# A chunk's second sums are cast behind the copy of its first product group, a half-down's last weights behind its two copies

## Chip, core and metric

One core of a Trainium2 chip runs the whole program. The metric is device microseconds (us) of one execution; the median of three runs of the kernel before is 1778.77 us (1778.58 to 1780.93).

## What is computed

A decoder trunk of two layers on 512 tokens of width 1024, in float32. Each layer has a half-step SwiGLU FFN, a mixer (gated linear attention in the first layer, stick-breaking attention in the second) and another half-step FFN; a final norm ends it. So there are four FFNs, and the change is in them alone:

```
def swiglu(h, w_gate, w_up, w_down):
    return (jax.nn.silu(h @ w_gate) * (h @ w_up)) @ w_down
...
    x = x + 0.5 * swiglu(rmsnorm(x, ffn1_norm[i]), ffn1_w_gate[i], ffn1_w_up[i], ffn1_w_down[i])
```

The inner width is 2816.

## The kernel before

**Splitting.** A float32 product is made of three passes: each operand is split into a high part (a cast to fp32r, on ScalarE, ACT) and a low part (operand minus high part, on VectorE, DVE), and TensorE (PE) multiplies high by high, low by high, high by low. For weights the cast is line 138 and writes `wh`, the subtraction is line 139 and writes `wl`. Both have four buffers of 128x1024 each, taken in turn; a piece of 128x512 has buffers of its own.

**Chunks of seven products.** For most of the inner width a chunk of 256 weight columns is multiplied with Strassen's scheme in seven products instead of eight (`seven`, lines 708 to 820). A product is 12 matmuls with 256 moving columns. A chunk needs two kinds of sums of its weights, both made on DVE: the first sums `s12` (lines 718 and 719) and the second sums `s34` (lines 724 and 725). It is two entries of a work list, the *feed*. The first entry, `body_1`, has units a11 (128x512), s12 and a2 (128x1024 each) and four products: 1 with a11 into the PSUM tile `ps_w`; ACT copies that to `ps_z` (line 761, the **z copy**); 2 with s12 into `ps_q`; 3 with s12, added onto `ps_w`, so it may not begin before the z copy has read `ps_w`; 4 with a2, added onto `ps_z`. The second entry, `body_2`, has the unit s34 and three products: 5 with s34 onto `ps_w`, 6 with s34 onto `ps_q`, 7 with a2 onto `ps_w`. Products 5, 6 and 7 each wait until ACT has copied the earlier content out (lines 769 for 5, 765 for 6, 783 for 7). DVE or ACT then gate the result (lines 743 and 746), and it is split (lines 838 and 839).

**Downs and half-downs.** The product with `w_down` is cut into *downs* (`down`, one unit of 128x1024, 24 matmuls with 512 columns) or, for groups 1 and 3 of an FFN, into two *half-downs* each (`seven_down`, lines 358 to 454), which are seven products of two parts m=0 and m=1 with six matmuls each, 12 together. Their `body_1` has units a11 (128x512), s12 and a2 (128x1024, cast as two pieces of 128x512, `wh<-rawd`), and runs: w (a11 into `ps_w` of both m, each followed by a copy to `ps_z`, line 412: the **two copies**), q (s12), t2 (s12 onto `ps_w`, behind the copies; line 400 then adds it to x on DVE), z (first piece of a2 onto `ps_z`). `body_2` (s34): t3 onto `ps_w`, behind the addition of line 400 that reads it, then a copy of each m (line 439, `u3`); b22 onto `ps_q`; t4 (second piece of a2) onto `ps_w`, where m=0 waits for the first of those copies and m=1 for the second.

**Order of the feed in one FFN.** Call the chunks 1 to 18 and the half-downs A to D. The matmuls of an FFN run so, the first entries and the last downs left out: chunks 1, 2, 3, a down, 4, a down, 5, 6, half-down **A**, 7, 8, 9, half-down **B**, a down, 10, a down, 11, a down, 12, a down, 13, 14, half-down **C**, 15, 16, half-down **D**, a down, 17, 18, downs. In the first FFN chunk 2 begins at 73.44 us, chunk 6 at 122.66, A at 132.46, B at 170.7, C at 248.25, chunk 16 at 267.0, D at 277.1 and the down behind it at 286.6.

**Who decides the order.** The code asks for splits ahead of use: when an entry starts, `Feed.start` splits the units of that entry and of the next two, as long as they have at most four units of 128x1024 together, views the next four and issues loads for the next six. A scheduler then puts each engine's instructions into one order at build time, by priority; instructions made under `ahead()` get a higher one. Each engine takes its list in that order and waits at an instruction whose inputs are not there. Weights are loaded by SyncE (SP): `raw` (1 MB, two buffers) for chunks, `rawd` (512 KB, two buffers) for downs and half-downs. A half-down takes both `rawd` buffers, and the load of the next down's weights is issued when DVE has read the last piece of a2 from one of them (line 139).

Of the kernel before, what the change touches and what calls it, by code (L numbers as in the profile page):

```python
# [46 lines left out]
def decoder(ctx: ExitStack, tc: tile.TileContext, a: dict, out: bass.AP):  # L47
# [60 lines left out]
    class Entry:  # L108
# [12 lines left out]

        def split(self):
            if self.W is None:
                self.W = []
                for r, (_, _, n, m) in zip(self.view(), self.units):
                    few = n * m < 1024
                    if few:

                        h, l = (
                            st["few"].tile([P, n * m], F32R, tag="v" + t, bufs=1, name="w" + t) for t in "hl"  # L130
                        )
                    else:
                        h, l = (wp.tile([P, n * m], F32R, tag="w" + t, bufs=4, name="w" + t) for t in "hl")
                    h, l = (t.rearrange("p (n m) -> p n m", m=m) for t in (h, l))
                    pieces = r if isinstance(r, tuple) else (r,)
                    for i, part in enumerate(pieces):
                        k = slice(i * n // len(pieces), (i + 1) * n // len(pieces))
                        st["cut"] = nc.scalar.copy(h[:, k], part).ins  # L138
                        nc.vector.tensor_tensor(out=l[:, k], in0=part, in1=h[:, k].bitcast(F32), op=ALU.subtract)  # L139
                    self.W.append((h, l))  # L140

    class Feed:
# [49 lines left out]
    def ahead():  # L192

        return tc.high_priority(4000)
# [163 lines left out]
    def seven_down(pool, w, r0, hs, part):  # L358
# [43 lines left out]
        def body_1(W):  # L402
            a11, s, v["a2"] = W
            ws, zs, qs = [], [], []
# [3 lines left out]
            for m in range(2):  # L408


                zs.append(psum("ps_z")[:, 0:H])
                nc.scalar.copy(zs[m], ws[m])
            yield
# [37 lines left out]

        units = [(lower, lambda t: halves()[0], 2, 256), (lower, sums_12, 4, 256), (lower, lambda t: halves()[1::2], 4, 256)]
        feed.q.append(Entry(units, body_1))
        feed.q.append(Entry([(lower, sums_34, 4, 256)], body_2))

    def back_tok(w, r0, nf, hs, done):
# [160 lines left out]
    class FFN:  # L617
# [90 lines left out]
        def seven(self, ch, group=None):  # L708
# [41 lines left out]
            def body_1(W):  # L750
# [9 lines left out]
                with ahead():  # L760
                    nc.scalar.copy(z, w)  # L761
                yield
# [57 lines left out]
            feed.q.append(Entry(units, body_1))  # L820
            feed.q.append(Entry([(ch, sums_34, KD, P)], body_2))

        def t_half(self, i, j):
# [58 lines left out]
        def evac_u(self, ps, group):  # L882
            t = self.tp.tile([P, T], F32, tag="t", name="t")
            if not self.normed:
                nc.vector.tensor_tensor(out=pair(t), in0=flat(ps), in1=pair(st["R"]), op=ALU.mult)
            nc.vector.tensor_tensor(
                out=pair(t), in0=flat(ps) if self.normed else pair(t), in1=pair(self.gates.pop(0)), op=ALU.mult
            )
            self.close(t, group)

# [1045 lines left out]
```

## Time and profile before

| | |
|---|---|
| median of three runs | 1778.77 us |
| the profiled execution's own time | 1778.36 us |
| span of its instructions | 1776.4 us, 31377 instructions |
| PE busy | 1755.4 us, 99% |
| DVE busy | 1509.6 us, 85% |
| ACT busy | 1079.6 us, 61% |
| granted TensorE clock | 0.999 of full |

The execution's time is 1.94 us longer than its span. Busy means that at least one instruction is in flight; matmuls overlap, so PE counts as busy through most short delays, and delays are better seen in the rows of waits and in the length of a product. PEld is the loading of PE's weights, which runs beside the matmuls and waits for the same things.

### The profile page before, as it was taken

The page shows a single profiled execution, that of the slowest core. Times are in us where ns is not written, and L with a number is a line of the kernel's source. Part 1 is how long each engine was busy: PE and PEld are TensorE (multiplying, and loading weights), DVE is VectorE, ACT ScalarE, POOL GpSimd, SP SyncE. Part 2 cuts the span into 40 slices and gives each one's busy share as a digit, 9 for nine tenths or more (in the row PEclk, how much of TensorE's full clock was granted, in tenths as well). Part 3 has the DMA queues.
Part 4 walks back from the last instruction along what each step waited for, and adds up shares of the span by engine and source line. Part 5 has one row for each costly group of instructions (what it writes and reads, how often), then busy time and mean ns, then how long its engine had stood idle before and what let it go on. Part 6 is the DMA issues. An engine that isn't in the chain of part 4 may idle for free.

```text
span 1776.4 us, 31377 instructions
## 1 busy us (share of the span) xinstructions
PE 1755.4 (99%) x12714; PEld 1630.6 (92%) x12714; DVE 1509.6 (85%) x2474; ACT 1079.6 (61%) x1883; POOL 55.6 (3%) x77
## 2 busy tenths in 40 slices
PE   9999999999999999999999999999999999999998
PEld 8999999889888899999889999999888888999997
DVE  8999797786888989888798988967898679997986
ACT  7556556554655566555655555655888755565564
POOL 0000000200000000000000000010000000000000
PEclk9999999999999999999999999999999999999999
DMA  5543435422123433444434344342212234434441
GB/s 167 154 120 119 125 102 148 113 66 73 54 90 100 121 117 120 119 120 125 129 95 133 102 125 126 118 120 83 84 48 72 72 95 131 126 104 123 120 138 52
DMA packets 186388, 193.14 MB, mean 109 GB/s; under 512 B 4930, under 2 KB 171124, under 8 KB 186244
## 3 DMA queue, kind: packets, MB, share of 16 engines
q1 hardware_dynamic: 177760, 175.91, 31.7%
q0 software_dynamic: 8240, 14.95, 4.6%
q8 instruction: 99, 1.62, 0.4%
q14 instruction: 45, 0.37, 0.1%
q10 hardware_dynamic: 244, 0.29, 0.0%
HBM read 175.17 MB, written 2.10 MB: 100 GB/s over the span
## 4 chain that ended last, share of the span: by engine, by line
PE 60%; DVE 30%; ACT 5%; issue 3%; DMA 2%; SPq 0%; DVEq 0%; ACTq 0%
PE ps_w L733 13%; PE ps_d L80 12%; DVE wl L139 9%; PE ps_f L80 7%; PE ps_q L733 6%; PE ps_t L80 4%; PE ps_z L733 3%; PE ps_b L80 3%; PE ps_w L394 3%; ACT wh L138 2%; DVE x L400 2%; DVE hl L839 1%; PE ps_q L394 1%; DVE ts L848 1%; PE ps_z L1424 1%
## 5 line engine op out<-in xcount | busy, mean ns | idle before, releaser
L139 DVE TENSOR_TENSOR wl<-raw,wh 128x1024 fp32r<-128x1024 f32 x241 | 255.5, 1061 | 59.4 <-ACT wh L138 58.8
L138 ACT CAST wh<-raw 128x1024 fp32r<-128x1024 f32 x241 | 221.6, 920 | 77.8 <-PE ps_f L80 22.6
L139 DVE TENSOR_TENSOR wl<-s,wh 128x1024 fp32r<-128x1024 f32 x176 | 214.6, 1219 | 50.7 <-ACT wh L138 50.7
L733 PE MATMUL ps_w<-th,wh 128*128 128x256 f32 x864 | 239.4, 277 | 6.3 <-ACT ps_z L761 6.3
L733 PE MATMUL ps_w<-th,wl 128*128 128x256 f32 x864 | 237.6, 275 | 0.0
L733 PE MATMUL ps_w<-tl,wh 128*128 128x256 f32 x864 | 237.6, 275 | 0.0
L138 ACT CAST wh<-s 128x1024 fp32r<-128x1024 f32 x176 | 184.1, 1046 | 69.6 <-DVE s L719 19.4
L733 PEld LDWEIGHTS ps_w<-th,wh 128*128 128x128 f32 x864 | 165.8, 192 | 9.5 <-ACT ps_z L761 9.4
L80 PE MATMUL ps_f<-xh,wh 128*128 128x512 f32 x432 | 166.4, 386 | 0.0
L733 PEld LDWEIGHTS ps_w<-tl,wh 128*128 128x128 f32 x864 | 165.9, 192 | 0.0
L733 PEld LDWEIGHTS ps_w<-th,wl 128*128 128x128 f32 x864 | 165.8, 192 | 0.0
L80 PE MATMUL ps_f<-xh,wl 128*128 128x512 f32 x432 | 164.2, 380 | 0.5 <-DVE wl L139 0.5
L80 PE MATMUL ps_f<-xl,wh 128*128 128x512 f32 x432 | 163.9, 379 | 0.0
L80 PE MATMUL ps_d<-hl,wh 128*128 128x512 f32 x416 | 158.0, 380 | 1.7 <-DVE hl L839 1.7
L80 PE MATMUL ps_d<-hh,wh 128*128 128x512 f32 x416 | 158.0, 380 | 0.5 <-ACT hh L838 0.5
L80 PE MATMUL ps_d<-hh,wl 128*128 128x512 f32 x416 | 157.7, 379 | 0.0
L139 DVE TENSOR_TENSOR wl<-rawd,wh 128x1024 fp32r<-128x1024 f32 (+1 forms) x100 | 96.1, 964 | 15.8 <-ACT wh L138 15.1
L138 ACT CAST wh<-rawd 128x1024 fp32r<-128x1024 f32 (+1 forms) x100 | 82.9, 845 | 39.4 <-PE ps_d L80 25.6
L345 POOL DMA_DIRECT2D x<-d x53 | 45.8, 888 | 1510.1 <-ACT d L344 832.2
L80 PEld LDWEIGHTS ps_f<-xl,wh 128*128 128x128 f32 x432 | 81.6, 189 | 11.5
L80 PEld LDWEIGHTS ps_f<-xh,wl 128*128 128x128 f32 x432 | 81.7, 189 | 11.3 <-DVE wl L139 0.9
L80 PEld LDWEIGHTS ps_f<-xh,wh 128*128 128x128 f32 x432 | 81.7, 189 | 10.8
(355 smaller groups left out, 5331.4 us busy)
## 6 DMA issues: line engine op xcount, KB each, us to landing
raw<-in_ffn_w_gate_dram SPq DMA_DIRECT2D x43, 1024.0 KB, 5.4
raw<-in_ffn_w_up_dram SPq DMA_DIRECT2D x43, 1024.0 KB, 5.4
rawd<-in_ffn_w_down_dram SPq DMA_DIRECT2D x84, 512.0 KB, 3.8
x<-d POOLq DMA_DIRECT2D x53, 256.0 KB, 4.6
raw<-in_gla_w_in_dram SPq DMA_DIRECT2D x12, 1024.0 KB, 5.4
raw<-in_sb_w_in_dram SPq DMA_DIRECT2D x16, 512.0 KB, 3.7
raw<-in_gla_w_out_dram SPq DMA_DIRECT2D x4, 1024.0 KB, 5.1
raw<-in_sb_w_in_dram SPq DMA_DIRECT2D x4, 1024.0 KB, 5.2
```

The costliest lines, as they stand in the source:

```text
L80: st["pe"] = nc.tensor.matmul(ps, l, r, start=first, stop=last).ins
L138: st["cut"] = nc.scalar.copy(h[:, k], part).ins
L139: nc.vector.tensor_tensor(out=l[:, k], in0=part, in1=h[:, k].bitcast(F32), op=ALU.subtract)
L345: nc.gpsimd.dma_start(xs[k], d, accum_op=ALU.add)
L394: st["pe"] = nc.tensor.matmul(ps, l_, r_, start=first and c + n == 0, stop=c == 1 and n == 2, skip_group_check=True).ins
L400: nc.vector.scalar_tensor_tensor(out=x, in0=ps, scalar=0.5, in1=x, op0=ALU.mult, op1=ALU.add)
L733: st["pe"] = nc.tensor.matmul(o, l_, r_, start=first and j + n == 0, stop=j == 3 and n == 2, skip_group_check=True).ins
L839: nc.vector.tensor_tensor(out=l, in0=t, in1=h.bitcast(F32), op=ALU.subtract)
L848: nc.vector.tensor_tensor(out=o, in0=p, in1=q, op=ALU.subtract)
L1424: nc.tensor.matmul(o_, l_, r_, start=first, stop=last, skip_group_check=True)
```

## The change

When `Feed.start` reaches the second entry of a chunk whose first entry follows the second entry of another chunk or half-down, it stops. That s34 is then split inside the chunk's own `body_1`, right after the z copy, and its cast is tied behind the z copy on ACT (`issue_after`). This holds for chunks 2, 3, 6, 7, 8, 9, 14, 15, 16 and 18 of each FFN. The unit a2 of a half-down is held back in the same way: `settle` splits it inside `body_1`, its casts tied behind the second of the two copies; entries behind a half-down that still waits for this are not split at that start. The two copies of a half-down now have the priority of `ahead()`, and so have the gating and split of the FFN's first, full products (`evac_u`), whose place in the lists is the same as before. No instruction is added or removed, and PE, SP and POOL keep their order.

```
         def __init__(self, units, body):
             self.units, self.body, self.W, self.views = units, body, None, None
+            self.second, self.v, self.held = False, None, None
...
-        def split(self):
+        def split(self, after=None):
             if self.W is None:
                 self.W = []
...
+                for i, (r, (_, _, n, m)) in enumerate(zip(self.view(), self.units)):
+                    if i == self.held:
+                        self.W.append(None)
+                        continue
+                    self.W.append(self.parts(r, n, m, after))
+
+        @property
+        def waits(self):
+            return self.held is not None and (self.W is None or self.W[self.held] is None)
+
+        def settle(self, after):
+            i = self.held
+            _, _, n, m = self.units[i]
+            self.W[i] = self.parts(self.view()[i], n, m, after)
+            return self.W[i]
+
+        def parts(self, r, n, m, after):
...
+                with tc.issue_after(after) if after is not None else ExitStack():
+                    nc.scalar.copy(h[:, k], part)
+                nc.vector.tensor_tensor(out=l[:, k], in0=part, in1=h[:, k].bitcast(F32), op=ALU.subtract)
...
-            for e in self.q[i : i + 3]:
+            for n, e in enumerate(self.q[i : i + 3]):
+                if e.v is not None and "copied" not in e.v and self.q[i + n - 2].second:
+                    break
                 used += sum(n * m >= 1024 for _, _, n, m in e.units)
                 if used > 4:
                     break
                 e.split()
+                if n and self.q[i + n - 1].waits:
+                    break
...
         def body_1(W):
-            a11, s, v["a2"] = W
+            a11, s = W[0:2]
...
-                nc.scalar.copy(zs[m], ws[m])
+                with ahead():
+                    copied = nc.scalar.copy(zs[m], ws[m]).ins
+            v["a2"] = v["first"].settle(copied)
             yield
...
                 with ahead():
-                    nc.scalar.copy(z, w)
+                    v["copied"] = nc.scalar.copy(z, w).ins
+                v["second"].split(v["copied"])
                 yield
```

Three places show how the lists move. All are in the first FFN; names end in numbers of their own, which differ between the two programs.

The first is ACT's list around the z copy of chunk 6. Before, with `s34_1348` the second sums of chunk 6, `s12_1426` the first sums of half-down A and `rawd_1316` its a11:

```order
L138 CAST wh_1420<-s34_1348 128x1024
L743 ACTIVATE o0_1354<-o0_1354 128x256
L743 ACTIVATE o1_1355<-ps_w_1351 128x256
L138 CAST wh_1538<-s12_1426 128x1024
L761 COPY ps_z_1479<-ps_w_1477 128x256
L138 CAST wh_1534<-rawd_1316 128x512
L765 COPY o1_1481<-ps_q_1478 128x256
L769 COPY o0_1480<-ps_w_1477 128x256
```

And the same stretch in the changed program, where `s34_1470` are the second sums of half-down A:

```order
L743 ACTIVATE o0_1354<-o0_1354 128x256
L743 ACTIVATE o1_1355<-ps_w_1351 128x256
L789 COPY ps_z_1475<-ps_w_1473 128x256
L156 CAST wh_1491<-s34_1348 128x1024
L156 CAST wh_1534<-rawd_1316 128x512
L794 COPY o1_1477<-ps_q_1474 128x256
L156 CAST wh_1538<-s12_1422 128x1024
L798 COPY o0_1476<-ps_w_1473 128x256
L156 CAST wh_1542<-s34_1470 128x1024
```

The casts of s34 and of the half-down's s12 stood ahead of the z copy and now stand behind it; the s12 cast now stands ahead of the copy of line 798 (769 before), for which product 5 waits.

The second place is DVE's list before half-down A. Before, from the subtraction of chunk 6's s34 on, with both pieces of a2 (`wl_1543`) among the rows:

```order
L139 TENSOR_TENSOR wl_1421<-s34_1348,wh_1420 128x1024
L724 TENSOR_TENSOR s34_1608<-raw_1429 128x512
L139 TENSOR_TENSOR wl_1539<-s12_1426,wh_1538 128x1024
L139 TENSOR_TENSOR wl_1535<-rawd_1316,wh_1534 128x512
L725 TENSOR_TENSOR s34_1608<-raw_1429,s12_1552 128x512
L718 TENSOR_TENSOR s12_1688<-raw_1555 128x512
L719 TENSOR_TENSOR s12_1688<-s12_1688,raw_1555 128x512
L139 TENSOR_TENSOR wl_1543<-rawd_1316,wh_1542 128x512
L746 TENSOR_TENSOR o0_1480<-ps_z_1479,o0_1354 128x256
L139 TENSOR_TENSOR wl_1543<-rawd_1424,wh_1542 128x512
```

In the changed program the pieces of a2 (`wl_1624`) come much later. From the subtraction of s34 (`wl_1492`) on, the rows ahead of those shown are three subtractions of 128x1024 (s34 of chunk 6, s12 and s34 of A), three operations of 128x512 and four of 128x256; then come:

```order
L718 TENSOR_TENSOR s12_1684<-raw_1549 128x512
L771 TENSOR_TENSOR o0_1476<-o0_1476,o0_1354 128x256
L771 TENSOR_TENSOR o1_1477<-ps_w_1473,o1_1355 128x256
L719 TENSOR_TENSOR s12_1684<-s12_1684,raw_1549 128x512
L870 TENSOR_TENSOR hl_1581<-o0_1476,hh_1580 128x512
L870 TENSOR_TENSOR hl_1599<-o1_1477,hh_1598 128x512
L724 TENSOR_TENSOR s34_1734<-raw_1549 128x512
L156 TENSOR_TENSOR wl_1624<-rawd_1316,wh_1623 128x512
L156 TENSOR_TENSOR wl_1624<-rawd_1420,wh_1623 128x512
L424 SCALAR_TENSOR_TENSOR x4_85<-ps_q_1629,x4_85 128x256
L424 SCALAR_TENSOR_TENSOR x5_86<-ps_q_1629,x5_86 128x256
L424 SCALAR_TENSOR_TENSOR x0_81<-ps_w_1605,x0_81 128x256
```

Counted from the subtraction of s34 as the first, the first piece of a2 was the 8th; now it is the 18th, behind the gating and split of chunk 6.

The third place is ACT's list in half-down D. Before, `rawd_3277` are the weights of the down that follows D, `raw_3325` and `s12_3457` belong to chunk 17:

```order
L138 CAST wh_3453<-rawd_3277 128x1024
L412 COPY ps_z_3476<-ps_w_3462 128x256
L838 CAST hh_3449<-o1_3331 128x512
L412 COPY ps_z_3478<-ps_w_3469 128x256
L138 CAST wh_3523<-raw_3325 128x512
L138 CAST wh_3527<-s12_3457 128x1024
L439 COPY u3_3538<-ps_w_3462 128x256
L439 COPY u3_3538<-ps_w_3469 128x256
L138 CAST wh_3531<-raw_3325 128x1024
```

Now, with the two pieces of a2 (`wh_3470`) behind the second copy, and `rawd_3273` the weights of the following down:

```order
L435 COPY ps_z_3468<-ps_w_3459 128x256
L156 CAST wh_3470<-rawd_3145 128x512
L156 CAST wh_3470<-rawd_3268 128x512
L156 CAST wh_3523<-raw_3321 128x512
L463 COPY u3_3538<-ps_w_3452 128x256
L156 CAST wh_3519<-rawd_3273 128x1024
L156 CAST wh_3527<-s12_3447 128x1024
L156 CAST wh_3531<-raw_3321 128x1024
L463 COPY u3_3538<-ps_w_3459 128x256
```

The cast of the following down's weights stood ahead of the two copies and now stands behind the first `u3` copy, and three casts stand ahead of the second. In B of all FFNs the rows behind the two pieces are the cast of chunk 10's a11, the cast of the following down's weights, the cast of chunk 10's s12, and then both `u3` copies; in D of the third FFN all three casts stand ahead of both.

More of the change, by code (lines that the diff above doesn't have):

```diff
@@ L453, in seven_down @@
         feed.q.append(Entry(units, body_1))
+        feed.q[-1].held = 2
+        v["first"] = feed.q[-1]
         feed.q.append(Entry([(lower, sums_34, 4, 256)], body_2))
+        feed.q[-1].second = True
+        v["last"] = feed.q[-1]
     def back_tok(w, r0, nf, hs, done):
@@ L885, in evac_u @@
                 nc.vector.tensor_tensor(out=pair(t), in0=flat(ps), in1=pair(st["R"]), op=ALU.mult)
[L886 to L889, printed above, removed]
+            with ahead():
+                nc.vector.tensor_tensor(
+                    out=pair(t), in0=flat(ps) if self.normed else pair(t), in1=pair(self.gates.pop(0)), op=ALU.mult
+                )
+                self.close(t, group)
         def close(self, t, group):
```

29 lines of the change are left out of this document (14 added, 15 removed).

## The prediction

> **What bounds the kernel.** First the page, its engines and its chain; then PE's waits; then one stretch.
>
> ```profile
> PE 1755.4 (99%) x12714; PEld 1630.6 (92%) x12714; DVE 1509.6 (85%) x2474; ACT 1079.6 (61%) x1883; POOL 55.6 (3%) x77
> PE 60%; DVE 30%; ACT 5%; issue 3%; DMA 2%; SPq 0%; DVEq 0%; ACTq 0%
> PEld ps_w L733 <- ACT ps_z L761: 9.4, 16, 1.3
> PEld ps_w L394 <- ACT ps_z L412: 0.5, 1, 0.5
> 106.00:146.00 40.00, 39.84 (x335) 39.01 (x334) 39.77 (x69) 23.93 (x42) 0.85 (x1) 1.00 0.37 112
> ```
>
> PE is the bound of the whole, with few waits; the first kind is the one that the change aims at. But DVE has 30% of the chain, and the window shows where: from 106 to 146 us (columns: length, then busy time of PE, PEld, DVE, ACT, POOL, then clock) DVE is busy for 39.77 of 40 us. There PE has little to wait for only because DVE works ahead. ACT has room.
>
> One of the 16 waits, at chunk 2 of the first FFN:
>
> ```profile
> 75.99 1.04 ACT L138 CAST wh<-s 128x1024 fp32r<-128x1024 f32 x1
> 76.92 0.38 ACT L761 COPY ps_z<-ps_w 128x256 f32<-128x256 f32 x1
> 77.35 0.19 PEld L733 LDWEIGHTS ps_w<-th,wh 128*128 128x128 f32 x1 [1.26 <-ACT ps_z L761]
> 77.36 0.38 PE L733 MATMUL ps_w<-th,wh 128*128 128x256 f32 x1 [1.07 <-ACT ps_z L761]
> 77.57 0.28 PE L733 MATMUL ps_w<-th,wl 128*128 128x256 f32 x1
> 80.30 1.34 PE ps_w L733 x12
> ```
>
> ACT casts sums first, the z copy follows, and product 3 begins when it ends. A product takes 1.34 us undisturbed, a chunk or half-down 7 x 1.34 = 9.38. The first matmul after a wait takes 0.38 instead of 0.28.
>
> **The gain.** Waits of 9.4 and 0.5 us, and 17 restarts of 0.1: **11.6 us** if all go. That the z copy comes free is read from ACT's new list: behind chunk 6's last gates it comes first, and the casts that stood ahead follow. So I count all 11.6.
>
> **What the moved work costs.** Nothing is added; each instruction moves. Steps on an engine are shorter than durations, since the next begins before the last ends. DVE and ACT:
>
> ```profile
> 133.99 0.68 DVE L839 TENSOR_TENSOR hl<-o,hh 128x512 fp32r<-128x512 f32 x1
> 134.59 1.22 DVE L139 TENSOR_TENSOR wl<-s,wh 128x1024 fp32r<-128x1024 f32 x1
> 135.72 0.68 DVE L839 TENSOR_TENSOR hl<-o,hh 128x512 fp32r<-128x512 f32 x1
> 136.33 0.75 DVE L400 SCALAR_TENSOR_TENSOR x<-ps_q,x 128x256 f32<-128x256 f32 x2
> 136.99 0.41 DVE L400 SCALAR_TENSOR_TENSOR x<-ps_w,x 128x256 f32<-128x256 f32 x1
> 272.21 1.16 ACT L138 CAST wh<-rawd 128x512 fp32r<-128x512 f32 x2
> 278.29 1.05 ACT L138 CAST wh<-rawd 128x1024 fp32r<-128x1024 f32 x1 [0.40 <-DMA rawd<-in_ffn_w_down_dram]
> 279.24 0.37 ACT L412 COPY ps_z<-ps_w 128x256 f32<-128x256 f32 x1
> ```
>
> So DVE steps are 1.13 us for 128x1024, 0.60 for 128x512, 0.33 for 128x256; ACT steps 0.95 for a large cast, 0.54 for a half one (two in 1.16), 0.27 for a copy of 0.37.
>
> *DVE behind a late s34.* In an undisturbed chunk the z copy starts about 0.2 us after product 2 begins:
>
> ```profile
> 143.19 0.28 PE L733 MATMUL ps_q<-th,wh 128*128 128x256 f32 x1
> 143.38 0.36 ACT L761 COPY ps_z<-ps_w 128x256 f32<-128x256 f32 x1 [0.29 <-PE ps_w L733]
> 123.26 0.69 DVE L719 TENSOR_TENSOR s<-s,raw 128x512 f32<-128x512 f32 x1
> 123.86 1.22 DVE L139 TENSOR_TENSOR wl<-s,wh 128x1024 fp32r<-128x1024 f32 x1
> ```
>
> Count from the chunk's start. The copy runs from 1.34+0.19 to 1.9, the s34 cast to about 2.9, and DVE's subtraction can start at 2.95. At chunk 6 (start 122.66) DVE was there at 123.86, that is at 1.2; now it stands still for some 1.7 us, in a stretch where it has no time over. The subtraction ends at 4.2 and product 5 needs it at 5.36+0.11, so s34 itself is not late. What is late is what DVE does next.
>
> *Front of a half-down: z and t3.* From the start of that subtraction to the end of a2's first piece, DVE has 18 instructions: three of 128x1024, eight of 128x512, six of 128x256, and the piece itself with 0.69: 3.39+4.8+2.0+0.69 = 10.9, and some 0.2 in small waits. From 2.95 that ends at 14.0 of the chunk, which is 4.6 of the half-down. Product z needs its low part at 4.02+0.11. **Wait 0.4.** Then come a2's second piece (0.60), two additions for q and the one that reads `ps_w` (0.33+0.33+0.41): 4.5+0.60+1.07 = 6.2, and t3, due at 5.36+0.4, waits another **0.35**. With a restart that is 0.85. It holds for A and C (behind chunks 6 and 14) and for D (behind 16): 12 places, **10.2 us**. Bounds: 0 if DVE's instructions elsewhere overlap better, 1.3 if each small wait grows by 0.2. B is spared: there DVE gates before s34's subtraction, and from that (at 3.5 of chunk 9) to the first piece's end stand three large, seven of 128x512, two of 128x256 and the piece, 3.39+4.2+0.66+0.69 = 8.9, which ends at 12.4, or 3.1 of B, ahead of z.
>
> *Back of B and D: a load.* The load of the next down's weights can be issued only when a2's pieces are read. In the trace that is so to the hundredth, and the cast of those weights is already waited for:
>
> ```profile
> 274.03 0.69 DVE L139 TENSOR_TENSOR wl<-rawd,wh 128x512 fp32r<-128x512 f32 x1
> 274.74 6.25 SPq L105 DMA_DIRECT2D rawd<-in_ffn_w_down_dram  x3
> DMA to landing us min/median/max: 3.4/3.5/4.0
>   DMA rawd<-in_ffn_w_down_dram: 4.0, 8
> 281.44 1.05 ACT L138 CAST wh<-s 128x1024 fp32r<-128x1024 f32 x1 [0.47 <-PE ps_w L394]
> 283.50 0.37 ACT L439 COPY u<-ps_w 128x256 f32<-128x256 f32 x1 [1.01 <-DVE x L400]
> 284.15 0.37 ACT L439 COPY u<-ps_w 128x256 f32<-128x256 f32 x1 [0.28 <-PE ps_w L394]
> 285.29 0.28 PE L394 MATMUL ps_w<-nh,wh 128*128 128x256 f32 x1
> 285.96 0.28 PE L394 MATMUL ps_w<-nh,wh 128*128 128x256 f32 x1
> ```
>
> (The third row is of the three loads at D; the fourth says that ACT waited for such loads 8 times in all, 4.0 us: once in each B and D.) Before, the load was issued 2.4 us ahead of D's start. Now a2's first piece is read inside the half-down, 3.2 us after its start at the earliest (copies to 1.9, cast to 2.5, subtraction to 3.2). Behind the cast that waits for the landing, ACT's list has the `u3` copies, and t4 waits for them: its first part was due at 285.29, 8.04 after the half-down's start plus small waits, its second 0.67 later.
>
> In B: read at 3.2, landed at 6.75 (3.5), cast and s12 cast to 8.7, first copy done at 9.15. t4 is due at 8.04: **1.1**, with restart 1.15, four times: 4.6.
> In D of three FFNs: read at 4.6, landed at 8.1, three large casts (2.85) to 11.0, second copy done at 11.3 with the engine's hand-over. Due at 8.71+0.8 = 9.5: **1.8**, 1.9 with restart, three times 5.7. In D of the third FFN even the first copy is behind the three casts; it is due 0.67 earlier: 2.6. Together **12.9 us**; at the least, with DVE never late, 4 x 1.13 + 3 x 1.4 + 2.1 = 10.8; at the most, with landings of 4.0 and another 0.3 of DVE, 19.
>
> The Trainium skill ("DMA: Bandwidth & Descriptors", the two cost components of a transfer) gives a load a fixed 2.0 us plus its bytes at 436 GB/s, which for these 512 KB makes an estimate of 3.2. The rows say 3.4 to 4.0, and they decide; by the page the eight waits would come out about 0.3 us shorter each, 2 us in all.
>
> *Two smaller ones.* In the first and third FFN chunk 2's z copy is late (its gates were late), so the copy for product 5 ends 0.2 after its due time, and chunk 3's z copy stands behind three casts that need DVE's late gating: 0.4. With restarts 0.65, twice. In chunk 9 the cast of the half-down's s12 stands ahead of product 5's copy and makes it late by about 0.2, four times. Together **2.1 us**, between 0 and 4.
>
> **Sum.** -11.6 + 10.2 + 12.9 + 2.1 = **+13.6 us**. The profiled execution took 1778.36 (span 1776.4 and 1.94 around it), 0.4 below the median; 1778.77 + 13.6 = 1792.4, say **1792**.
>
> **Rivals.**
> (a) *The gain alone.* For it speaks that the aimed-at waits are the largest kind of PE wait and that the new list frees the z copy. It needs the loads of B and D to hide, which the order of the list and 3.4 us to landing deny. 1778.8-11.6 = 1767.
> (b) *Fronts hide, loads do not.* DVE catches up before z, since it had idle time before chunk 8 and in the downs; only the floor of the loads and the small ones stay: -11.6+10.8+2.1 = +1.3, 1780.
> (c) *DVE becomes the bound.* New idle time of about 1.5 us at each of chunks 6, 8, 14 and 16 is passed to PE in full, because DVE was full: 16 x 1.5 = 24 in the place of the fronts' 10.2: 1806. Against it: after chunk 7 DVE arrives late anyway, so idle times do not add up.
> (d) *The change misses its aim*: casts that depend on DVE stand ahead of the z copies elsewhere too, as in chunk 3, and the 11.6 stay: 1804.
> (e) *PE loses its clock in the new waits.* The rows show 1.00 through waits of 1.26 us. If each of B's and D's waits cost two products at half rate, 8 x 2.7 = 22 us more: 1814. The Trainium skill ("TensorE: Matmul & The Clock Gate", Part 1) says that the clock halves after an idle window of about 3.4 us. By that rule my waits of at most 2.6 stay below it; no run here shows it.
>
> **Chances.** Forecast 0.66 (1783 to 1801), (a) 0.07, (b) 0.14, (c) 0.08, (d) 0.03, (e) 0.02. A measurement of this kernel tells about 0.2%, 3.6 us, from no change. Faster by more: (a) and a little of (b), 0.08. Within: most of (b), 0.11. Slower: 0.81. The range reaches into (b) at its lower end, the fronts at nearly nothing, and up to the upper bounds of the loads: 1780 to 1802.
>
> **What would show it.** In the profile after, the waits of PE for line 761's z copy (now line 789) should be nearly gone except at chunk 3. PE should wait in half-downs A, C and D for `wl` of the a2 pieces and then for the additions to x, and at the end of B and D for the `u` copies, with ACT's cast of `rawd` waiting for a DMA just before. DVE should stand idle ahead of s34's subtraction in chunks 6, 8, 14 and 16. If the `u` copies are not waited for, the load was issued or landed earlier than I think and the forecast is too slow by up to 13 us; if the z copies still are, the gain is wrong.

## The result, and the profile after

The changed kernel takes **1792.33 us** (median of 6 runs, 1790.51 to 1796.07), the kernel before in the same set 1779.91 us. The ratio is **1.0073** with a 95% interval of 1.006 to 1.0087: slower by 13 us, between 10.7 and 15.5. The forecast was 1792. Of the six executions three took 1790.51 to 1790.66 us, the profiled one 1793.99, and two, whose granted clock was 0.998 and 0.997 where the others had 0.999, 1795.06 and 1796.07.

Two lines of the page after, engines and chain:

```profile
PE 1762.3 (98%) x12714; PEld 1635.2 (91%) x12714; DVE 1506.2 (84%) x2474; ACT 1072.5 (60%) x1883; POOL 55.6 (3%) x77
PE 66%; DVE 21%; ACT 6%; DMA 3%; issue 2%; DVEq 0%; ACTq 0%; SPq 0%
```

DVE has lost a third of its share of the chain, 30% to 21%, and the kernel is slower all the same. The waits of PE say why (waited for: us in total, times, longest):

```profile
PE ps_w L416 <- ACT u L463: 12.7, 8, 1.9
PE ps_z L416 <- DVE wl L157: 1.5, 6, 0.3
PE ps_w L761 <- ACT ps_z L789: 0.4, 2, 0.2
```

The z copy is now line 789. These rows are PE's own, and before they had:

```profile
PE ps_w L733 <- ACT ps_z L761: 6.3, 16, 1.1
```

So of 6.3 us in 16 places 0.4 in two places are left. (The prediction's 9.4 us are from the rows of the weight loads, PEld; there 1.2 us in four places are left.) In its stead t4 waits in eight half-downs for the `u3` copies (now line 463).

One of the eight is B of the first FFN, which begins at 172.22 us. ACT, then DVE, then the queue of SP, then PE:

```profile
174.03 1.14 ACT L156 CAST wh<-rawd 128x512 fp32r<-128x512 f32 x2
175.07 0.62 ACT L156 CAST wh<-raw 128x512 fp32r<-128x512 f32 x1
179.37 1.05 ACT L156 CAST wh<-rawd 128x1024 fp32r<-128x1024 f32 x1 [3.68 <-DMA rawd<-in_ffn_w_down_dram]
180.32 1.04 ACT L156 CAST wh<-s 128x1024 fp32r<-128x1024 f32 x1
181.27 0.64 ACT L463 COPY u<-ps_w 128x256 f32<-128x256 f32 x2
```

```profile
174.68 1.29 DVE L157 TENSOR_TENSOR wl<-rawd,wh 128x512 fp32r<-128x512 f32 x2 [0.24 <-ACT wh L156]
```

```profile
175.40 0.37 SPq L105 DMA_DIRECT2D rawd<-in_ffn_w_down_dram  x1
```

```profile
181.68 0.38 PE L416 MATMUL ps_w<-nh,wh 128*128 128x256 f32 x1 [1.26 <-ACT u L463]
181.90 0.28 PE L416 MATMUL ps_w<-nh,wl 128*128 128x256 f32 x1
```

The chain is to be read from its end. PE starts t4 when the first copy has ended. Both copies stand behind a cast of the next down's weights and a cast behind that one, and the first of these stood still for 3.68 us until its load had landed. The copies themselves could have run earlier: the first begins 9.05 us after the start of B here, and 6.28 us after it in the last version below, where these casts do not stand ahead of it. The load was issued at 175.40, when DVE had read the first held piece of a2 (its subtraction, the first of the two from 174.68 on, takes 0.69 us). The Trainium skill ("PSUM — Partial Sum Buffer", Engine vs sequencer instructions) calls ScalarE's queue a strict FIFO; the 3.68 us in which ready copies stayed behind a waiting cast agree with that.

For sums over all places the text below uses delays by product: the time from one matmul's start to the next beyond 0.112 us, added up over the 12 matmuls of a product (24 and 0.216 us for a down), all four FFNs together, places above 0.11 us. The numbers are worked out from the starts of the PE rows of each profiled execution. "Chunk 3" is product 3 of the chunks, for which the z copy is due, and so on.

| kernel | chunk 3 | chunk 5 | t2 | z | t3 | t4 | downs | sum | median us |
|---|---|---|---|---|---|---|---|---|---|
| before | 10.8 | 0 | 0.8 | 0 | 0 | 0 | 0 | 11.6 | 1778.8 to 1779.9 |
| the change | 1.7 | 1.7 | 0 | 3.1 | 3.5 | 14.8 | 0 | 24.7 | 1792.3 |

The difference of the sums is 13.1 us. The profiled executions differ by 15.6 (1793.99 and 1778.36), but 1.9 of that lie in the first 11 us, ahead of any instruction that moved: there the execution of after kept half pace longer (last section).

### The profile page after: what moved, and what is told of

Its sections match the earlier page's. It is cut to its first block, busy times and chain, and to the rows that moved or that the text cites. A ratio compares the mean times of both kernels' runs of the same rounds, so it can differ in the third digit from the quotient of the medians.

```text
span 1792.1 us, 31323 instructions
## 1 busy us (share of the span) xinstructions
PE 1762.3 (98%) x12714; PEld 1635.2 (91%) x12714; DVE 1506.2 (84%) x2474; ACT 1072.5 (60%) x1883; POOL 55.6 (3%) x77
## 4 chain that ended last, share of the span: by engine, by line
PE 66%; DVE 21%; ACT 6%; DMA 3%; issue 2%; DVEq 0%; ACTq 0%; SPq 0%
PE ps_w L761 17%; PE ps_d L80 12%; PE ps_q L761 8%; PE ps_f L80 7%; DVE wl L157 6%; PE ps_t L80 4%; PE ps_z L761 4%; PE ps_b L80 3%; ACT wh L156 3%; PE ps_w L416 3%; DMA rawd<-in_ffn_w_down_dram 2%; DMA raw<-in_ffn_w_gate_dram 1%; DVE ts L879 1%; PE ps_z L1456 1%; DVE xn L863 1%
## 5 line engine op out<-in xcount | busy, mean ns | idle before, releaser
L80 PEld LDWEIGHTS ps_f<-xh,wh 128*128 128x128 f32 x432 | 81.9, 189 | 10.6
```

Source lines behind the costliest of these rows:

```text
L80: st["pe"] = nc.tensor.matmul(ps, l, r, start=first, stop=last).ins
```

## The experiments

Each ratio compares with the kernel before, timed in the same set. The median of the kernel before was 1778.8 to 1779.9 us in these sets, so between kernels of different sets a difference of 1 us says nothing; the intervals of the ratios tell more.

### Each part alone

**The chunk part alone**: a2 is split with the rest of its entry again, without `held` and `settle`, and the two copies lose `ahead()`.

```
-            a11, s = W[0:2]
+            a11, s, v["a2"] = W
...
-                with ahead():
-                    copied = nc.scalar.copy(zs[m], ws[m]).ins
-            v["a2"] = v["first"].settle(copied)
+                nc.scalar.copy(zs[m], ws[m])
...
-        feed.q[-1].held = 2
```

> Only the chunk part of the change: s34 is still split behind the z copy, but a half-down's a2 is split ahead of it as in the kernel before, and its two copies have no raised priority. Theory 1 (the half-down part makes the losses: at the end of B and D through the late load of the next down's weights, whose cast stands ahead of the u3 copies, about 16 us; in front of z and t3 through the late low part of a2, about 5 us): t4 waits in no half-down, z waits in none, the 9.4 us of waits for the z copy are nearly gone, and of the losses only those at chunk 3 and chunk 9 stay, 1 to 2 us. The time is 1779.9 - 11.6 + 2 = 1770 us. Theory 2 (the late split of s34 leaves DVE idle before it, and this lateness alone makes the waits in front of z and t3): t4 doesn't wait, z and t3 do, and the time is 1775 to 1780.

Measured: **1786.32 us**, ratio 1.0041 (1.0028 to 1.0053), 7 us slower than before and 16 above what theory 1 gave. Both theories of that text fell. The z copies are free and t4 doesn't wait, as expected, but there are three new waits:

```profile
PE ps_w L416 <- ACT ps_z L434: 5.3, 7, 1.2
PE ps_w L416 <- DVE x L422: 2.6, 6, 0.4
PE ps_w L758 <- DVE wl L157: 2.2, 4, 1.3
```

The first is t2 of B and D, which waits for the two copies (7.5 us by product), the second t3, the third product 5 of the chunk behind A. ACT in D of the first FFN shows what the copies stand behind:

```profile
281.50 1.07 ACT L156 CAST wh<-rawd 128x1024 fp32r<-128x1024 f32 x1 [0.68 <-DMA rawd<-in_ffn_w_down_dram]
282.48 0.62 ACT L866 CAST hh<-o 128x512 fp32r<-128x512 f32 x1
282.99 0.63 ACT L434 COPY ps_z<-ps_w 128x256 f32<-128x256 f32 x2
```

It is the cast of the next down's weights again, here ahead of the two copies instead of the `u3` copies. (In the two kernels below in which this cast stands behind the two copies, t2 waits nowhere.)

**The half-down part alone**: s34 of a chunk is split where it was before.

```
-                if e.v is not None and "copied" not in e.v and self.q[i + n - 2].second:
-                    break
...
-                v["second"].split(v["copied"])
```

> Only the half-down part of the change: a2 is held until behind the two copies, which have raised priority, but s34 of the chunks is split where it was before. Theory 1: the 16 waits for the z copy are back (9.4 us and restarts), t4 waits at the end of B and D in all four FFNs, 14 to 17 us, and since DVE no longer stands still before s34 it is early for the low part of a2, so that z does not wait: 1779.9 + 16 - 0.5 = about 1795.5 us. Theory 2 (the lateness of the load is hidden unless DVE is late as well): t4 waits much shorter, 1780 to 1786. Theory 3 (the held a2 alone makes z wait): 1800.

Measured: **1797.87 us**, ratio 1.011 (1.0096 to 1.0124); the profiled execution, 1802.5, was the longest of its four.

```profile
PE ps_w L414 <- ACT u L461: 12.0, 8, 2.1
PE ps_w L759 <- ACT ps_z L787: 8.7, 13, 2.2
```

t4 waits as in the whole change (14.4 us by product), so its cause is in this part. z waits nowhere, as theory 1 said: that wait needs the late s34 too. But t3 waits 0.36 us in all twelve half-downs A, C and D (4.3 us) with no late s34. Its additions stand behind both held pieces in DVE's list, which start 3.30 us after the start of A in the first FFN. That place alone is not enough: in the kernel below that also puts s34's first subtraction behind the pieces, the place is the same, the pieces start at 2.47, and t3 waits nowhere. Chunk 8 waits longer for its z copy than before, 6.3 us against 1.7. The two parts are no sum: 7.4 alone and 18.9 alone make 13.0 together. By the tables the 7.5 us at t2 go when a2 is held, chunk 3's 15.3 go when s34 is late, and t3's wait, in each part, is there once.

Two of these waits cost more than their length. At once after one, and 1.0 us after the other, the matmuls fall to half pace for 3.41 us, 0.43 us from start to start for 512 columns in place of 0.216, and the granted clock (the last figure but two) is 0.50:

```profile
181.79 0.38 PE L414 MATMUL ps_w<-nh,wh 128*128 128x256 f32 x1 [2.07 <-ACT u L461]
184.91 0.63 PE L80 MATMUL ps_d<-hh,wh 128*128 128x512 f32 x1
185.34 0.63 PE L80 MATMUL ps_d<-hh,wl 128*128 128x512 f32 x1
183.00:186.00 3.00, 3.00 (x10) 2.55 (x10) 3.00 (x8) 1.05 (x1) 0.00 (x0) 0.50 0.62 183
```

This is B of the first FFN; the other is chunk 8 of the last, after a wait of 2.20 us. The half pace costs 1.7 and 1.6 us. It lies in this execution's sums, and the down behind B of the first FFN, which the table below gives 1.3 us, waits for nothing: it runs at half pace.

### The cast that waits for its load

**The next down's cast behind the `u3` copies**, on top of the whole change. The down behind B or D is not split at the start of `body_2`, but in it, tied behind the second copy; the entry behind it follows.

```
                 e.split()
+                if self.q[i].tail and self.q[i + 1].units[0][0].few:
+                    break
...
-                nc.scalar.copy(pair(u3[:, m]), flat(ws[m]))
+                copied = nc.scalar.copy(pair(u3[:, m]), flat(ws[m])).ins
                 add(m, 1, 1, pair(u3[:, m]))
+            if feed.q[feed.pos].units[0][0].few:
+                feed.q[feed.pos].split(copied)
+                feed.q[feed.pos + 1].split()
...
-        v["last"] = feed.q[-1]
+        feed.q[-1].tail = True
```

> The whole change, and one more: the down behind a half-down is split inside that half-down, its cast tied behind the second u3 copy. Only the rows of the u3 copies in B and D move, ahead of the cast of the next down's weights; the load of those weights is issued as late as before. Theory 1 (t4 waits because the cast that waits for the load stands ahead of the u3 copies in ACT's list): the t4 waits (8, 12.7 us as PE counts them, about 16 with restarts) vanish, the down behind waits 0.2 us at most for its low part, z still waits in six half-downs, and the time is 1792.3 - 16 + 2 = 1778 us. Theory 2 (the late load itself costs, whatever stands behind it): the wait moves from t4 to the start of the down, and the time stays at 1788 to 1792.

Measured: **1779.69 us**, ratio 1.0003 (0.9994 to 1.0012). The t4 waits are gone, all 14.8 us; the downs behind B and D wait 2.3 in their stead. ACT in D of the first FFN, which begins at 276.32:

```profile
283.48 0.38 ACT L466 COPY u<-ps_w 128x256 f32<-128x256 f32 x1 [2.73 <-PE ps_w L419]
284.11 0.37 ACT L466 COPY u<-ps_w 128x256 f32<-128x256 f32 x1 [0.25 <-PE ps_w L419]
284.52 1.05 ACT L157 CAST wh<-rawd 128x1024 fp32r<-128x1024 f32 x1
```

The cast begins 8.20 us after the half-down's start, against 8.32 in the whole change (288.09, with a start at 279.77). So the load is as late as there; only the place of its cast, with the casts queued behind it, has changed, and with it nearly all of the loss. Theory 1 holds, theory 2 for 2.3 us of 14.8.

**Also s34's first subtraction behind the pieces of a2.**

```
-            for e in self.q[i : i + 4]:
+            for e in self.q[i : i + (3 if self.q[i].held else 4)]:
                 e.view()
...
-                nc.vector.tensor_tensor(out=l[:, k], in0=part, in1=h[:, k].bitcast(F32), op=ALU.subtract)
+                low = nc.vector.tensor_tensor(out=l[:, k], in0=part, in1=h[:, k].bitcast(F32), op=ALU.subtract)
+            if len(pieces) == 2:
+                st["settled"] = low.ins
...
+                with tc.issue_after(st["settled"]) if "settled" in st else ExitStack():
-                nc.vector.tensor_tensor(out=s[:, 0:4], in0=t[:, 0:4, 0:P], in1=t[:, 0:4, P:], op=ALU.subtract)
+                    nc.vector.tensor_tensor(out=s[:, 0:4], in0=t[:, 0:4, 0:P], in1=t[:, 0:4, P:], op=ALU.subtract)
```

> As the kernel with the down's cast behind the u3 copies, and also: a chunk's first subtraction for s34 (128x512, on DVE) that was listed just ahead of the a2 pieces of half-downs A, C and D in some FFNs is tied behind the second of these pieces; some sums of the next chunk move behind them too. Theory 1 (z waits 0.4 us and t3 0.27 us more in six of the twelve half-downs because that one row of 0.6 us stands ahead of a2's low part): z waits nowhere, and the time is 4 to 5 us below that of the kernel without this edit, about 1773 to 1774. Theory 2 (DVE is full, and what moves behind comes late instead): z no longer waits, but the next chunk waits for its sums, and the time is the same or longer.

Measured: **1776.41 us**, ratio 0.9983 (0.9974 to 0.9992), 3.3 below the kernel without this edit. z and t3 wait nowhere (6.6 us less), and 3.6 come back: the downs wait 5.0 us instead of 2.3, the chunks 2.6 instead of 1.7. Both theories have their part.

### Holding nothing

**The chunk part and the raised copies, a2 not held**: as the chunk part alone, but the two copies keep `ahead()`.

```
+            a11, s, v["a2"] = W
...
+                with ahead():
+                    copied = nc.scalar.copy(zs[m], ws[m]).ins
-            v["a2"] = v["first"].settle(copied)
...
-        feed.q[-1].held = 2
```

> The chunk part of the change and, of the half-down part, only the raised priority of the two copies; a2 is split ahead as in the kernel before. In the kernel with the chunk part alone, PE waited 7.5 us for the two copies (product t2 of B and D), 4.3 for t3 of A and C, 4.4 at product 5 of chunks 7 and 9. Theory 1 (the copies are late only because casts that depend on a late DVE stand ahead of them in ACT's list, and priority cures that; the rest stays): t2's waits vanish, no t4 wait comes, the time is 1786.3 - 7.5 = 1779 us, and the holding of a2 is what costs in the whole change. Theory 2 (ACT itself is late, whatever its order): t2's waits stay, 1785 or more.

Measured: **1779.83 us**, ratio 1.001 (1.0001 to 1.0019). The time is that of theory 1, its reason is not: t2 still waits 5.7 us of 7.5. ACT in B of the first FFN:

```profile
172.01 1.06 ACT L156 CAST wh<-rawd 128x1024 fp32r<-128x1024 f32 x1 [0.31 <-DMA rawd<-in_ffn_w_down_dram]
172.97 0.62 ACT L435 COPY ps_z<-ps_w 128x256 f32<-128x256 f32 x2
```

Priority did not move the copies past the cast. What fell were t3 (4.3 to 1.3) and part of the others. From the whole change this kernel differs only in that a2 is not held: 1779.8 against 1792.3. So the hold costs some 12.5 us: it frees t2 (5.7) and adds, above all, the 14.8 at t4 and the 3.1 at z.

**The next down's cast behind the two copies**, a2 still not held:

```
+                if n == 2 and self.q[i].half and e.units[0][0].few:
+                    break
                 e.split()
...
                     copied = nc.scalar.copy(zs[m], ws[m]).ins
+            if feed.q[feed.pos + 1].units[0][0].few:
+                feed.q[feed.pos + 1].split(copied)
...
-        v["first"] = feed.q[-1]
+        feed.q[-1].half = True
```

> As the kernel with the chunk part and the raised copies (1779.8 us), and the cast of the next down's weights is tied behind the second of the two copies in B and D; a2 is not held, so the load of these weights keeps its early issue. In the kernel without this edit ACT's cast of rawd waits 0.3 us for its DMA right ahead of the two copies, and t2 waits 5.7 us in all eight half-downs B and D. Theory 1 (one cast, that of the next down's weights, makes both t2's waits without the hold and t4's waits with it, by standing ahead of a PSUM copy): t2's waits go, t4 doesn't wait, and the time is 1779.8 - 5.7 = 1774 us. Theory 2 (DVE's late gating and the activations ahead of the copies hold them back): t2's waits stay above 3 us, 1777 or more.

Measured: **1782.59 us**, ratio 1.0017 (1.0008 to 1.0026). t2's waits are gone, as theory 1 said, but the time did not fall, since others came:

```profile
PE ps_w L419 <- DVE x L425: 4.6, 8, 1.1
PE ps_w L764 <- DVE wl L158: 2.6, 4, 1.6
```

The wait went to t3, 7.9 us by product. The same edit in the next kernel but one shows why, on DVE in D:

```profile
278.21 0.69 DVE L750 TENSOR_TENSOR s<-s,raw 128x512 f32<-128x512 f32 x1
278.82 1.22 DVE L158 TENSOR_TENSOR wl<-rawd,wh 128x1024 fp32r<-128x1024 f32 x1
279.95 0.75 DVE L425 SCALAR_TENSOR_TENSOR x<-ps_q,x 128x256 f32<-128x256 f32 x2
280.62 0.75 DVE L425 SCALAR_TENSOR_TENSOR x<-ps_w,x 128x256 f32<-128x256 f32 x2
```

The low part of the same weights, with sums of the next chunk, now stands ahead of the additions for which t3 waits.

**s34 late only in the chunks of w_up**, with the raised copies, a2 not held. These are 2, 6, 8, 14, 16 and 18, and all that waited before are among them.

```
-            feed.q[-1].second, feed.q[-1].v = True, v
+            feed.q[-1].second, feed.q[-1].v = True, v if group is not None else None
```

> As the kernel with the chunk part and the raised copies, but s34 is split late only in the chunks of w_up (2, 6, 8, 14, 16 and 18, those whose z copy was waited for before), and early as in the kernel before in chunks 3, 7, 9 and 15. Theory 1 (each late s34 makes DVE stand still for 1.5 us, and a chunk that gains nothing from it only pays): the waits at product 5 of chunks 7 and 9 and half or more of those of t3 go, the z copies of 2, 6, 8, 14 and 16 stay free, 6 us or more below the kernel with all late, 1771 to 1774. Theory 2 (DVE's total work sets the time in this stretch, its order only moves the wait): no faster than the kernel with all late, 1778 or more.

Measured: **1774.78 us**, ratio 0.9979 (0.9971 to 0.9988), 5.1 below the kernel with all chunks late. Product 5 of chunks 7 and 9 is free (3.6 us), t2 waits 2.2 instead of 5.7; chunk 9's z copy is late now, 1.4. Theory 1 holds for product 5 and for the z copies it names. It does not hold for t3 (1.4 against 1.3), the time is 0.8 above its range, and 3.5 us of the gain came at t2, which it did not name. With the next down's cast tied behind the two copies as above:

> As the kernel with s34 late in the chunks of w_up alone and the raised copies (1774.8 us), and the cast of the next down's weights tied behind the two copies, a2 not held. Theory 1: the 2.2 us of t2's waits go and nothing comes back, 1772.6 us, below all kernels so far. Theory 2 (the down's cast, now later, makes the down wait for its low part): the same or up to 2 us longer.

Measured: **1775.91 us**, ratio 0.9984 (0.9975 to 0.9993). t2 is free, t3 waits 6.6: the rows shown above are from this kernel. The time is in theory 2's range, but not for its reason: the downs wait nowhere.

The limit to w_up on the kernel with a2 held, the down's cast behind the `u3` copies and s34 behind a2; its edit is the same line again:

```
+            feed.q[-1].second, feed.q[-1].v = True, v if group is not None else None
```

> As the kernel with a2 held, the next down's cast behind the u3 copies and s34's first subtraction behind the pieces of a2 (1776.4 us), but with s34 split late only in the chunks of w_up. Its remaining delays were 1.8 us at product 5 and 0.8 at product 3 of chunks 2, 3 and 9, and 5.0 us at the downs behind B and D, which wait for the low part of the late-loaded weights. Theory 1: those in chunks 3 and 9 go and DVE is earlier at the downs by the idle time of one chunk, so that a part of the 5.0 goes too: 1773 to 1775 us. Theory 2: the downs wait for the landing alone, not for DVE, and stay at 5.0: 1775 to 1776.

Measured: **1776.18 us**, ratio 0.9987 (0.9978 to 0.9996), no better than with all late (0.9983). The chunks' delays moved from product 5 to product 3 and grew from 2.6 to 4.3; the downs kept 4.0 of 5.0. Neither theory is borne out in full.

### A version below both kernels

s34 late in the chunks of w_up, a2 not held, the copies raised, and the next down's cast tied behind the second `u3` copy (the edit of the third experiment in `body_2`, with this condition).

```
+                if n and self.q[i + n - 1].tail and e.units[0][0].few:
+                    break
                 e.split()
...
+            if feed.q[feed.pos].units[0][0].few:
+                feed.q[feed.pos].split(copied)
+                feed.q[feed.pos + 1].split()
```

> As the kernel with s34 late in the chunks of w_up alone and the raised copies (1774.8 us), a2 not held and the load early, but with the cast of the next down's weights tied behind the second u3 copy instead of the second of the two copies. Theory 1 (in D of the kernel with the cast behind the two copies, its low part on DVE stood ahead of the additions to x for which t3 waits; behind the u3 copies it has nobody to delay): no t2 waits, t3 waits of D no longer than 0.3 each, the down's low part in time because its load is early: 1772 to 1773 us. Theory 2 (the sums of the next chunk, which stand ahead of the additions as well, are enough to delay t3, or the down waits for its low part as where a2 was held): 1775 to 1777.

Measured: **1772.69 us**, ratio **0.996** (0.9947 to 0.9974), 7 us below the kernel before and 20 below the change. ACT in its B of the first FFN:

```profile
175.97 0.38 ACT L465 COPY u<-ps_w 128x256 f32<-128x256 f32 x1 [3.84 <-PE ps_w L419]
176.59 0.37 ACT L465 COPY u<-ps_w 128x256 f32<-128x256 f32 x1 [0.25 <-PE ps_w L419]
176.86 1.05 ACT L157 CAST wh<-rawd 128x1024 fp32r<-128x1024 f32 x1
```

The copies now wait for PE, not PE for them. The time is the one that theory 1 gave, its account is only half right: t2 is free, but t3 of D still waits 0.48 us in three FFNs, where 0.3 was the most it allowed, and the down behind D of the last FFN 0.5. Nor is it shown that this edit gained anything over the kernel with s34 late in the chunks of w_up alone: the sums of delays are 5.1 and 5.4, the profiled executions took 1773.53 and 1773.45, and the intervals of the two ratios overlap a little. What is shown is that both are faster than the kernel before. The sums over all places, as in the table above:

| kernel | chunk 3 | chunk 5 | t2 | z | t3 | t4 | downs | sum | median us |
|---|---|---|---|---|---|---|---|---|---|
| chunk part alone | 0.7 | 4.4 | 7.5 | 0 | 4.3 | 0 | 0 | 16.9 | 1786.3 |
| half-down part alone | 15.3 | 0 | 0 | 0 | 4.3 | 14.4 | 1.3 | 35.3 | 1797.9 |
| change, down's cast behind u3 | 0.6 | 1.1 | 0 | 3.1 | 3.5 | 0 | 2.3 | 10.6 | 1779.7 |
| that, s34 behind a2 | 0.8 | 1.8 | 0 | 0 | 0 | 0 | 5.0 | 7.6 | 1776.4 |
| chunk part, copies raised | 0.7 | 3.9 | 5.7 | 0 | 1.3 | 0 | 0 | 11.6 | 1779.8 |
| that, cast behind two copies | 1.5 | 5.0 | 0 | 0 | 7.9 | 0 | 0 | 14.3 | 1782.6 |
| w_up only, copies raised | 1.5 | 0.3 | 2.2 | 0 | 1.4 | 0 | 0 | 5.4 | 1774.8 |
| that, cast behind two copies | 1.4 | 0.3 | 0 | 0 | 6.6 | 0 | 0 | 8.2 | 1775.9 |
| w_up only, a2 held, both tied | 4.0 | 0.3 | 0 | 0 | 0 | 0 | 4.0 | 8.2 | 1776.2 |
| w_up only, cast behind u3 | 1.4 | 0.6 | 0 | 0 | 2.6 | 0 | 0.5 | 5.1 | 1772.7 |

(In the row of the half-down part, chunk 3 includes 0.4 us at product 4, and 3.3 us of the sum are matmuls at half pace. Without them the sum is 20.4 above that of the kernel before, near the 18.9 of the medians.)

## Why the prediction was right, point by point

The time came out at the forecast, and by its mechanisms. That it agrees to less than 1 us is luck: the fronts were 3.6 us less than forecast, the loads 1.9 more and the small terms 1.2 more, which nearly cancels, and the median of the six executions lies between two groups of them.

**The gain, 11.6.** Measured 11.6: the 10.8 at product 3 of the chunks and the 0.8 at t2, as they stand in the first table, are gone but for 0.28 at chunk 2 of the first FFN and 0.35 at chunk 8 of the last, which are counted below with the small terms. The half-down part alone, where s34 is early, has the z copies' waits back. The runs add what the text did not see: the chunk part has this gain without the 0.8 only at the price of new waits at t2, because the cast of the next down's weights stays ahead of the copies there.

**Fronts of half-downs, 10.2.** Measured 6.6 (z 3.1, t3 3.5). The step that failed is "It holds for A and C (behind chunks 6 and 14) and for D (behind 16): 12 places". z waits in six of the twelve, 0.51 each, where the text had 0.4 and a restart; in the other six not at all. (The text's own figures, an end at 4.6 and a need at 4.13, give 0.5 and not 0.4; it then went on with 4.5, which is the end that was measured.) The 18 instructions were counted in A of the first FFN, and the lists of the others are not the same. DVE after, in A of the first FFN and in A of the second:

```profile
135.62 1.35 DVE L870 TENSOR_TENSOR hl<-o,hh 128x512 fp32r<-128x512 f32 x2
136.90 0.68 DVE L752 TENSOR_TENSOR s<-raw 128x512 f32<-128x512 f32 x1
137.50 1.29 DVE L157 TENSOR_TENSOR wl<-rawd,wh 128x512 fp32r<-128x512 f32 x2
```

```profile
685.80 0.69 DVE L870 TENSOR_TENSOR hl<-o,hh 128x512 fp32r<-128x512 f32 x1
686.40 0.69 DVE L157 TENSOR_TENSOR wl<-rawd,wh 128x512 fp32r<-128x512 f32 x1
```

The row of line 752 is missing in the second, and its 0.6 us decide: the first piece ends at 4.50 us of the half-down in the one (3.81+0.69), at 3.83 in the other, and z needs it at 4.13. Moving that row away, with some sums of the next chunk, freed z in all places (the fourth experiment). t3 waits in all twelve, 0.36 where z waits and 0.21 or 0.22 elsewhere; the half-down part alone shows that t3's wait needs no late s34.

DVE does stand still ahead of the late s34, as forecast. Chunk 6 of the first FFN:

```profile
124.97 0.69 DVE L747 TENSOR_TENSOR s<-s,raw 128x512 f32<-128x512 f32 x1
127.20 1.22 DVE L157 TENSOR_TENSOR wl<-s,wh 128x1024 fp32r<-128x1024 f32 x1 [1.55 <-ACT wh L156]
```

**Back of B and D, 12.9.** Measured 14.8: B 6.9 (forecast 4.6), D 7.9 (forecast 8.3). Issue came where it was said, 3.18 us after B's start (said 3.2). What was mis-sized is the landing, "landed at 6.75 (3.5)". The 3.5 was read at D; the same trace had the loads issued just ahead of B, which landed after 3.54, 3.75, 3.67 and 4.22 us. After the change the casts start 7.15, 7.75, 7.28 and 7.20 us after the start of B in the four FFNs, that is 3.97 to 4.56 after the issue. t4's delays there, 1.52, 2.12, 1.66 and 1.58, are these starts less 5.63 or 5.62 each time: a landing later by a tenth costs PE a tenth. In D of three FFNs three casts stand between, as forecast, with delays of 1.96 to 2.09 (forecast 1.9). In D of the third FFN only two do: the cast of chunk 17's a2 comes behind both copies, not ahead of them as the prediction and the section on the change have it.

```profile
1166.55 1.04 ACT L156 CAST wh<-s 128x1024 fp32r<-128x1024 f32 x1
1167.50 0.64 ACT L463 COPY u<-ps_w 128x256 f32<-128x256 f32 x2
1168.03 1.05 ACT L156 CAST wh<-raw 128x1024 fp32r<-128x1024 f32 x1
```

So its 2.6 came out at 1.75: one cast less (0.95), and DVE read a2 at 3.86 of the half-down, not at 4.6; against that, t4 was due earlier too, since z did not wait. ACT in B of the second FFN, which begins at 721.15:

```profile
728.89 1.05 ACT L156 CAST wh<-rawd 128x1024 fp32r<-128x1024 f32 x1 [4.27 <-DMA rawd<-in_ffn_w_down_dram]
730.79 0.64 ACT L463 COPY u<-ps_w 128x256 f32<-128x256 f32 x2
```

**Two smaller ones, 2.1.** Measured 3.3: chunk 2 0.85, chunk 3 0.88, chunk 9 0.98, and chunk 8 of the last FFN 0.64, which the text did not have.

**The rivals.** The gain alone (1767) would have needed the loads to hide; t4's 14.8 us deny it. Fronts that hide (1780) are denied by their 6.6 us. That the change misses its aim (1804) is denied by the freed z copies. DVE as the bound (1806) would have passed 16 stops of 1.5 us on in full; the fronts cost 6.6. But the kernels without the loads' cost show its trace: where t4 is free, product 5, t3 and the downs wait together for 1.7 to 12.9 us, by the rows in large part for DVE.

The lost clock (1814) did not come in the profiled execution of the change: its longest wait of PE is 1.86 us, and the matmuls after the wait at 181.68 follow each other in 0.11 us again from the second on. It is not dead, though. In the half-down part alone, waits of 2.07 and 2.20 us did halve the pace, for 1.7 and 1.6 us each. So in these traces pace was kept after waits of up to 1.86 us and lost after both of the longer ones, well below the 3.4 that rival (e) went by. By these two, the waits of 2.6 us that it thought safe were not. The change's two executions with the lower clock may have lost time in the same way; they have no profile, so that is not shown.

No experiment took the raised priority of `evac_u` away, whose order is the same with it and without. A third buffer for `rawd`, which would let the load be issued early with a2 held, was not tried.

Open is why the loads in B landed after 3.94 to 4.54 us, where those ahead of B in the trace before took 3.54 to 4.22. In both a second load is issued 0.6 us behind, so that does not tell them apart.

## What to carry to other kernels

When an order of work is moved to free one wait, look where the operation that waits for a load ends up in its engine's list: whatever stands behind it inherits the load's latency, and here one cast, with those queued behind it, cost 5.7 us ahead of one pair of copies, 14.8 ahead of the next and 0.5 to 5.0 behind both. Tie that operation behind what the busiest engine needs next, and move only the work that frees a wait. Count the rows of the list at every place where a term is applied; a list that reads alike in one layer may lack a row in the next, as it did twice here. And a long wait can cost more than its length: look at the pace of the matmuls behind it.

## What the runs showed that was not expected

The first matmuls of a program run at half pace for a time that differs from one execution to the next. PE at the start, after and then before:

```profile
9.02 1.06 PE L1759 MATMUL ps_f<-xh,wh 128*128 128x512 f32 x2
9.88 0.84 PE L1759 MATMUL ps_f<-xl,wh 128*128 128x512 f32 x2
```

```profile
7.81 0.59 PE L1727 MATMUL ps_f<-xh,wh 128*128 128x512 f32 x2
8.24 0.60 PE L1727 MATMUL ps_f<-xl,wh 128*128 128x512 f32 x2
```

Two matmuls of 512 columns take 0.86 us from start to start (9.02 to 9.88) in the one, 0.43 in the other (7.81 to 8.24). In the profiled executions of the change and of the chunk part this lasts to 10.4 and 10.5 us, in that of before to 4.7, and it makes 1.9 us between the spans of before and after. The granted clock of the first 20 us of the change reads 1.00 all the same (the last figure but two):

```profile
0.00:20.00 20.00, 19.03 (x88) 16.24 (x89) 12.06 (x29) 13.58 (x28) 0.70 (x6) 1.00 0.99 288
```

The reason lies in the trace: its first record of the clock stands at 10.36 us (4.65 before, 10.47 in the chunk part), and the column prints 1.00 for a stretch without a record. Where there are records the column agrees with the pace, as with the 0.50 in the half-down part alone. So at the start of a program the pace of the matmuls, not the clock column, tells whether PE is at full speed. The Trainium skill ("TensorE: Matmul & The Clock Gate", Part 1) says that PE starts at half clock until it has been busy for one window of about 3.4 us and that this varies from run to run; the half pace and its change from run to run agree with the rows. The 3.4 us cannot be read at the start, but both stretches at half pace in the half-down part alone last 3.41 us.
